# Scores inside the chunks of a gated linear recurrence: two full products for a pair of chunks in place of four partial ones

## The chip, the cores and the metric

The kernel runs on one core of a Trainium2 chip. The metric is the device time of one execution in microseconds (us). Before the change three runs gave 1615.14, 1615.44 and 1616.7 us, a median of 1615.44 us.

## The reference, cut to what matters

The kernel computes one encoder layer for 1024 tokens of width 1024, in float32: a recurrence branch with four heads, an attention branch with eight heads, a gated merge and a convolutional feed-forward network. The change lies in the recurrence, which runs over each head in both directions in chunks of 64 tokens:

```python
def gla_chunkwise(q, k, v, g):
    ...
    qd = q * jnp.exp(b)
    kd = k * jnp.exp(-b)
    A = jnp.einsum('bhncd,bhnsd->bhncs', qd, kd)
    mask = jnp.tril(jnp.ones((C, C), dtype=bool))
    A = jnp.where(mask, A, 0.0)
    intra = jnp.einsum('bhncs,bhnse->bhnce', A, v)
    ...
    inter = jnp.einsum('bhncd,bhnde->bhnce', qd, S_prev)
    return (intra + inter).reshape(B, H, L, dv)
```

A second call with the time axis flipped gives the backward direction, and the two results are added.

## The kernel before, in words

The program goes through stages: the first norm and two projections (to about 80 us), the recurrence of the four heads (`hg_proj` and `hg_rec`, to about 378 us), the rotary projections of the attention branch (`rope_unit`, names rk and rq), attention, the merge, and the feed-forward network with its down projection.

`hg_rec` (line 289) holds a head's tokens as eight pairs of chunks, 128 tokens each. For each direction it forms the scaled queries `qds[d]` and keys `kds[d]` (128 features by 1024 tokens), turns the keys round (`kt`, line 332), multiplies them with the values (`u`, line 338) and builds the states on VectorE (`R`, line 347, and `st`, line 349). Then come two blocks `b` of four pairs each. In each block TensorE forms the scores (lines 359 to 362), VectorE masks them and builds the 128 by 128 matrix `A` of each pair, which holds both directions (lines 365 to 370), and TensorE multiplies `A` with the values and adds the states' part in `po` (lines 376 and 378). A norm over `po` (`sq`, `hss`, `rs_h`, lines 379 to 386), a turn on TensorE (`ot`, line 389) and a copy (`oT`, line 390) end the block. There are four heads, so eight such blocks and 32 pairs.

The scores of a pair are four products before. Line 359 multiplies the backward keys of all 128 tokens with the backward queries of the first 64, line 360 the forward keys of all 128 with the forward queries of the last 64; both write the tile `a1`. Lines 361 and 362 multiply 64 keys with 64 queries: the forward direction inside the first chunk and the backward direction inside the second, into the two halves of the partitions of `a2`. The profile calls both tiles `a`. One product of the program in plain float32 is two loads and two matmuls in the profile.

The masked copies and sums on VectorE:

```python
V.copy_predicated(A, mask1..., a1.rearrange("p i a b -> p i (a b)"))
V.copy_predicated(at, mask2..., a2)
for r in (slice(0, CH), slice(CH, P)):
    V.tensor_tensor(out=A[r, :, r], in0=A[r, :, r], in1=at[r], op=ALU.add)
```

The tiles `kt`, `u`, `a1`, `a2` and `ot` share one tag "t" of three buffers in PSUM, so that each of them waits until the tile three places earlier has been read. The order of instructions on each engine is set when the program is built, by a scheduler that simulates the program on a timeline of its own; each engine then goes through its list in order. The work that stands between the steps of a head on TensorE is that of others: `hp` (line 92 to 94, the next head's projections), `v` and `sg` (values and gates), `gp` (line 257, branch gates of the attention stage) and `rk`.

At the end of the recurrence stands the rotary stage. Its projections `rk` take three PSUM buffers (tag "g"), and the fourth needs the first one back. For that ScalarE and VectorE have to copy out `rawk`, `sqk` and `vv` (lines 466, 468 and 77/78), and on VectorE the tables `cosq`, `cosk`, `sinq`, `sink` (lines 444 and 451) stand ahead of `vv`.

Of the kernel before, what the change touches and what calls it, by code (L numbers as in the profile page):

```python
# [10 lines left out]
F32 = mybir.dt.float32  # L11
# [6 lines left out]
P = 128  # L18
# [5 lines left out]
CH = 64  # L24
# [20 lines left out]
def hybrid_kernel(ctx: ExitStack, tc: tile.TileContext, x, gn, vec, cst, rope,  # L45
# [3 lines left out]
    V, S, T = nc.vector, nc.scalar, nc.tensor  # L49

    def pool(name, bufs, stack=ctx, **kw):
        return stack.enter_context(tc.tile_pool(name=name, bufs=bufs, reuse_waits="tile", **kw))
# [16 lines left out]
    mask1 = cs[:, C_M1:C_M1 + P].bitcast(U32)  # L69
    mask2 = cs[:, C_M2:C_M2 + CH].bitcast(U32)  # L70
# [147 lines left out]
    for d, (a, b) in enumerate(((V_LBF0, V_LBF1), (V_LBB0, V_LBB1))):  # L218
        w = slice(4 * d, 4 * d + 4)
# [16 lines left out]
    hps = pool("hps", 3, hg, space=PSUM)  # L236
# [52 lines left out]
    def hg_rec(h, q, ks, gs, vt, sg):  # L289
        e = slice((h % 2) * P, (h % 2 + 1) * P)  # L290
        chunks = lambda a: a.rearrange("p (a j) -> p a j", j=CH)
        first = lambda a: a.rearrange("p (a two j) -> p a two j", two=2, j=CH)[:, :, 0, :]
        qds, kds, decs = [], [], []
        for d in range(2):
            k, g = ks[d], gs[d]
            c = hp4.tile([P, L], F32, tag="c", name=f"c{h}{d}", bufs=2)
            for w in (slice(0, 512), slice(512, 1024)):
                V.tensor_tensor_scan(c[:, w], reset, g[:, w], 0.0, ALU.mult, ALU.add)
            tot = hp4.tile([P, 16], F32, tag="tot", name=f"tot{h}{d}", bufs=2)
            V.tensor_copy(tot, chunks(c)[:, :, CH - 1])  # L300
            c63 = tot.rearrange("p (a two) -> p a two", two=2)[:, :, 0:1].to_broadcast([P, 8, CH])
            if d == 0:
                b = c
                V.tensor_tensor(out=first(b), in0=first(c), in1=c63, op=ALU.subtract)
            else:
                b = g
                V.tensor_tensor(out=b, in0=g, in1=c, op=ALU.subtract)
                V.tensor_tensor(out=first(b), in0=first(b), in1=c63, op=ALU.add)
            dec = hp4.tile([P, 16], F32, tag="dec", name=f"dec{h}{d}", bufs=4)
            S.activation(dec, tot, AF.Exp)  # L310
            qd = hp3.tile([P, L], F32, tag="qd", name=f"qd{h}{d}", bufs=2)
            S.activation(qd, b, AF.Exp)
            V.tensor_tensor(out=qd, in0=qd, in1=q, op=ALU.mult)
            S.activation(b, b, AF.Exp, scale=-1.0)
            V.tensor_tensor(out=k, in0=k, in1=b, op=ALU.mult)
            qds.append(qd)
            kds.append(k)
            decs.append(dec)


        states = [[None] * NPAIR, [None] * NPAIR]
        for d in range(2):
            order = range(NPAIR) if d == 0 else range(NPAIR - 1, -1, -1)
            E0 = lambda p: decs[d][:, 2 * p + (1 if d else 0):2 * p + (1 if d else 0) + 1]
            E1 = lambda p: decs[d][:, 2 * p + (0 if d else 1):2 * p + (0 if d else 1) + 1]
            order = list(order)
            for b in range(2):
                grp = order[4 * b:4 * b + 4]
                pt = hps.tile([P, 4, P], F32, tag="t", name=f"kt{h}{d}{b}")
                kT = hp4.tile([P, 4, P], F32, tag="kT", name=f"kT{h}{d}{b}", bufs=2)  # L330
                for i, p in enumerate(grp):
                    T.transpose(pt[:, i, :], kds[d][:, p * P:(p + 1) * P], ident)
                S.copy(kT, pt)
                pu = hps.tile([P, 4, P], F32, tag="t", name=f"u{h}{d}{b}")
                for i, p in enumerate(grp):
                    if p == order[-1]:
                        break
                    T.matmul(pu[:, i, :], kT[:, i, :], vt[:, p, e], start=True, stop=True)
                for i, p in enumerate(grp):
                    if p == order[-1]:  # L340
                        break
                    nxt = order[4 * b + i + 1]
                    st = hp3.tile([P, P], F32, tag=f"st{d}", name=f"st{h}{d}{nxt}", bufs=8)
                    src = pu[:, i, :]
                    if states[d][p] is not None:
                        R = hp1.tile([P, P], F32, tag="R", name=f"R{h}{d}{p}", bufs=2)
                        V.tensor_tensor(out=R, in0=src, in1=states[d][p], op=ALU.add)
                        src = R
                    V.tensor_scalar(st, src, E1(p), E0(nxt), ALU.mult, ALU.mult)
                    states[d][nxt] = st  # L350

        oT = hp3.tile([P, L], F32, tag="oT", name=f"oT{h}", bufs=1)
        for b in range(2):
            a1 = hps.tile([P, 4, 2, CH], F32, tag="t", name=f"a1{h}{b}")
            a2 = hps.tile([P, 4, CH], F32, tag="t", name=f"a2{h}{b}")
            for i in range(4):
                o = (4 * b + i) * P
                w, f, s = slice(o, o + P), slice(o, o + CH), slice(o + CH, o + P)
                T.matmul(a1[:, i, 0, :], kds[1][:, w], qds[1][:, f], start=True, stop=True)
                T.matmul(a1[:, i, 1, :], kds[0][:, w], qds[0][:, s], start=True, stop=True)  # L360
                T.matmul(a2[0:CH, i, :], kds[0][:, f], qds[0][:, f], start=True, stop=True)
                T.matmul(a2[CH:P, i, :], kds[1][:, s], qds[1][:, s], start=True, stop=True)
            A = hp3.tile([P, 4, P], F32, tag="A", name=f"A{h}{b}", bufs=2)
            nc.gpsimd.memset(A, 0.0)
            V.copy_predicated(A, mask1.unsqueeze(1).to_broadcast([P, 4, P]),
                              a1.rearrange("p i a b -> p i (a b)"))
            at = a_tmp[b]
            V.copy_predicated(at, mask2.unsqueeze(1).to_broadcast([P, 4, CH]), a2)
            for r in (slice(0, CH), slice(CH, P)):
                V.tensor_tensor(out=A[r, :, r], in0=A[r, :, r], in1=at[r], op=ALU.add)  # L370
            po = hps.tile([P, 4, P], F32, tag="o", name=f"po{h}{b}", bufs=2)
            for i in range(4):
                p = 4 * b + i
                w = slice(p * P, (p + 1) * P)
                inter = [(qds[d][:, w], states[d][p]) for d in range(2) if states[d][p] is not None]
                T.matmul(po[:, i, :], A[:, i, :], vt[:, p, e], start=True, stop=False)
                for n, (a, s) in enumerate(inter):
                    T.matmul(po[:, i, :], a, s, start=False, stop=n == len(inter) - 1)
            sq = hp4.tile([P, 4, P], F32, tag="sq", name=f"sq{h}{b}")
            S.activation(sq, po, AF.Square)  # L380
            ss = hp4.tile([P, 4], F32, tag="ss", name=f"hss{h}{b}", bufs=2)
            V.tensor_reduce(out=ss, in_=sq, axis=AX.X, op=ALU.add)
            r = rstd_of(hp4, ss, P, 4, f"h{h}{b}")
            for i in range(4):
                V.scalar_tensor_tensor(out=sq[:, i, :], in0=po[:, i, :], scalar=r[:, i:i + 1],
                                       in1=sg[:, 4 * b + i, e], op0=ALU.mult, op1=ALU.mult)
            pt = hps.tile([P, 4, P], F32, tag="t", name=f"ot{h}{b}")
            for i in range(4):
                T.transpose(pt[:, i, :], sq[:, i, :], ident)
            S.activation(oT[:, b * 512:(b + 1) * 512], pt.rearrange("p a b -> p (a b)"), AF.Copy,  # L390
                         scale=vc[:, V_ON:V_ON + 1])
        nc.sync.dma_start(oa_d[h], oT)
# [23 lines left out]
    at = ExitStack()  # L416
# [22 lines left out]
    for n, col, sc in (("q", V_QG, HD ** -0.5), ("k", V_KG, 1.0)):  # L439
# [3 lines left out]
        s = rp.tile([P, 8, HD], F32, name=f"sin{n}")  # L443
# [173 lines left out]
    for h in range(HG_HEADS):  # L617
        t = slot_p(f"oal{h}", F32)
# [20 lines left out]
    for c in range(KT):  # L639
        wh, wl = weight_block(wab[c], f"ab{c}")  # L640
        sgt = []
        for n in range(2):
            t = slot_q(f"gl{n}{c}", F32)
# [3 lines left out]
        for half in range(2):  # L647
            w = slice(half * 512, (half + 1) * 512)
            for n in range(2):
                ps = yps.tile([P, 512], F32, tag="y", name=f"y{c}{half}{n}")  # L650
                for k in range(4):
                    kw = slice((4 * n + k) * P, (4 * n + k + 1) * P)
                    h, l = oab[4 * n + k]
# [71 lines left out]
    A, B, C, C1, C2, U2 = {}, {}, {}, {}, {}, {}  # L725
# [18 lines left out]
    def m1(j):  # L744
        A[j] = bank_a(f"pa{j}")
        product(A[j], wa[j], 0, "b11", True)

    def m2(j):
        B[j] = bank_b(f"pb{j}")
        product(B[j], wa[j], 1, "b21", True)  # L750
# [186 lines left out]
    for i in range(2):  # L937
        r = wpool.tile([P, 2, NH], F32, tag="raw", name=f"left{i}")
# [178 lines left out]
```

## Time and profile before

| what | value |
|---|---|
| median of three runs | 1615.44 us |
| time of the profiled execution | 1616.18 us |
| span of the profiled execution, first to last instruction | 1614.3 us |
| TensorE matmul busy | 1579.3 us, 98% |
| TensorE weight loads busy | 1334.1 us, 83% |
| VectorE busy | 1112.5 us, 69% |
| ScalarE busy | 768.0 us, 48% |
| mean granted TensorE clock | 0.993 of full |

The span is what the profile covers; the time of the execution is 1.88 us longer. Busy shares are means over stages with different limits, so a stage has to be read by itself. Matmuls overlap each other in the profile: what one costs is the step from its start to the start of the next, not its own duration.

### The profile page before, as it was taken

The page shows a single profiled execution, that of the slowest core. Times are in us where ns is not written, and L with a number is a line of the kernel's source. Part 1 is how long each engine was busy: PE and PEld are TensorE (multiplying, and loading weights), DVE is VectorE, ACT ScalarE, POOL GpSimd, SP SyncE. Part 2 cuts the span into 40 slices and gives each one's busy share as a digit, 9 for nine tenths or more (in the row PEclk, how much of TensorE's full clock was granted, in tenths as well). Part 3 has the DMA queues.
Part 4 walks back from the last instruction along what each step waited for, and adds up shares of the span by engine and source line. Part 5 has one row for each costly group of instructions (what it writes and reads, how often), then busy time and mean ns, then how long its engine had stood idle before and what let it go on. Part 6 is the DMA issues. An engine that isn't in the chain of part 4 may idle for free.

```text
span 1614.3 us, 21171 instructions
## 1 busy us (share of the span) xinstructions
PE 1579.3 (98%) x8376; PEld 1334.1 (83%) x8376; DVE 1112.5 (69%) x1632; ACT 768.0 (48%) x1204; POOL 35.3 (2%) x33
## 2 busy tenths in 40 slices
PE   8999999999999999999999989999999999999998
PEld 7988998888988888888788877788788888787887
DVE  5366465534758888888654288887888777967576
ACT  5375454513555666656432344544544444444432
POOL 0000000000000000000000052000000000000000
PEclk9999999999999999999999999999999999999999
DMA  5011111121110101102445111322222224685343
GB/s 204 27 41 38 53 40 49 64 78 54 46 60 27 46 33 40 47 26 99 167 140 195 53 59 66 104 98 98 98 98 98 103 106 147 212 296 186 100 122 104
DMA packets 59764, 150.34 MB, mean 93 GB/s; under 512 B 6161, under 2 KB 6417, under 8 KB 59666
## 3 DMA queue, kind: packets, MB, share of 16 engines
q1 hardware_dynamic: 59666, 148.99, 26.9%
q8 instruction: 66, 1.08, 0.3%
q14 instruction: 32, 0.26, 0.1%
HBM read 109.91 MB, written 39.06 MB: 92 GB/s over the span
## 4 chain that ended last, share of the span: by engine, by line
PE 85%; DVE 6%; DMA 5%; ACT 3%; issue 1%; SPq 0%; DVEq 0%; ACTq 0%
PE pa L741 13%; PE gp L257 10%; PE pc L741 6%; PE pv L578 4%; PE pb L741 3%; PE pt L567 3%; PE s L547 2%; PE hp L93 2%; PE s L548 2%; PE hp L94 2%; PE hp L92 2%; PE y L93 2%; PE y L94 2%; PE y L92 2%; PE wo L94 2%; PE wo L93 2%
## 5 line engine op out<-in xcount | busy, mean ns | idle before, releaser
L77 ACT CAST pth<-pt 128x512 fp32r<-128x512 f32 x128 | 71.1, 589 | 77.8 <-PE pt L567 77.5
L77 ACT CAST dz<-dr 128x512 fp32r<-128x512 f32 (+1 forms) x66 | 50.6, 767 | 102.1 <-PE da L94 35.8
L78 DVE TENSOR_TENSOR dz<-dr,dz 128x512 fp32r<-128x512 f32 (+1 forms) x66 | 56.9, 867 | 50.8 <-ACT dz L77 50.6
L78 DVE TENSOR_TENSOR ptl<-pt,pth 128x512 fp32r<-128x512 f32 x128 | 84.0, 683 | 10.3 <-ACT pth L77 9.9
L257 PE MATMUL gp<-uT1h,w_g 128*128 128x512 f32 x256 | 86.9, 398 | 0.0
L257 PE MATMUL gp<-uT0h,w_g 128*128 128x512 f32 x256 | 86.4, 400 | 0.0
L550 DVE TENSOR_REDUCE m<-s 128x1 f32<-128x1024 f32 x64 | 78.3, 1224 | 7.3 <-PE s L548 6.3
L553 ACT ACTIVATE p<-s,m 128x1024 f32<-128x1024 f32 x64 | 72.1, 1127 | 19.7 <-DVE m L550 19.7
L741 PE MATMUL pc<-c1t,wb 128*128 128x512 f32 x264 | 69.5, 398 | 5.5 <-ACT c1t L77 5.0
L741 PE MATMUL pa<-c0b,wa 128*128 128x512 f32 x264 | 68.9, 394 | 2.8 <-ACT wa L77 1.7
L741 PE MATMUL pb<-c0b,wa 128*128 128x512 f32 x264 | 68.7, 390 | 0.5 <-DVE ta L714 0.5
L567 PEld LDWEIGHTS pt<-cs,p 128*128 128x128 f32 x512 | 58.7, 140 | 12.0 <-issue 4.8
L741 PE MATMUL pa<-c1t,wb 128*128 128x512 f32 x264 | 67.9, 395 | 0.0
L567 PE MATMUL pt<-cs,p 128*128 128x128 f32 x512 | 66.9, 273 | 0.5 <-DVE p L555 0.5
L578 PE MATMUL pv<-pth,vv 128*128 128x256 f32 x256 | 65.1, 292 | 0.0
L741 PEld LDWEIGHTS pc<-c1t,wb 128*128 128x128 f32 x264 | 50.5, 192 | 17.0 <-ACT c1t L77 5.2
L77 ACT CAST wc<-r 128x1024 fp32r<-128x1024 f32 x22 | 23.1, 1052 | 86.1 <-PE pc L741 76.4
L578 PE MATMUL pv<-ptl,vv 128*128 128x256 f32 x256 | 62.5, 282 | 0.0
L741 PEld LDWEIGHTS pa<-c0b,wa 128*128 128x128 f32 x264 | 49.0, 188 | 15.4 <-ACT wa L77 3.2
L741 PEld LDWEIGHTS pa<-c1t,wb 128*128 128x128 f32 x264 | 50.1, 190 | 12.0 <-DVE c1t L78 0.4
L741 PEld LDWEIGHTS pb<-c0b,wa 128*128 128x128 f32 x264 | 49.5, 188 | 11.4 <-DVE ta L714 0.9
L868 DVE SCALAR_TENSOR_TENSOR cv<-c,vc,cv 128x1023 f32<-128x1023 f32 x44 | 56.3, 1279 | 2.6 <-ACT cv L867 2.6
(461 smaller groups left out, 4578.1 us busy)
## 6 DMA issues: line engine op xcount, KB each, us to landing
r<-in_wup_dram SPq DMA_DIRECT2D x44, 512.0 KB, 3.3
left_d<-cv SPq DMA_DIRECT2D x33, 512.0 KB, 3.2
dr<-left_d SPq DMA_DIRECT2D x66, 256.0 KB, 2.7
raw_g<-in_win_f_dram SPq DMA_DIRECT2D x16, 512.0 KB, 3.2
gate_d<-gt SPq DMA_DIRECT2D x32, 256.0 KB, 2.0
gl<-gate_d SPq DMA_DIRECT2D x16, 512.0 KB, 4.0
raw_h<-in_win_f_dram SPq DMA_DIRECT2D x12, 512.0 KB, 3.3
w<-in_wdown_dram SPq DMA_DIRECT2D x20, 256.0 KB, 5.4
```

The costliest lines, as they stand in the source:

```text
L77: S.copy(h, src)
L78: V.tensor_tensor(out=l, in0=src, in1=h.bitcast(F32), op=ALU.subtract)
L92: T.matmul(ps, ah, bh, start=first, stop=False, skip_group_check=more)
L93: T.matmul(ps, ah, bl, start=False, stop=False, skip_group_check=more)
L94: return T.matmul(ps, al, bh, start=False, stop=last, skip_group_check=more)
L257: yield T.matmul(ps, a[:, w], b[:, k, :], start=k == 0 and n == 0, stop=k == KT - 1 and n == 2)
L550: V.tensor_reduce(out=m, in_=s, axis=AX.X, op=ALU.max, negate=True)
L553: S.activation(pb, s, AF.Exp, bias=m, accum_out=z)
L567: pin(T.transpose(pt[:, i, :], pb[:, k * P:(k + 1) * P], ident))
L578: pin(T.matmul(pv, vv[pair // 2][:, k, :], pts[u][k // 4][n][:, k % 4, :, :], start=k == 0 and n == 0, stop=k == KT - 1 and n == 1))
L741: T.matmul(ps, a[:, k * P:(k + 1) * P], x[:, k, :], start=first and n == 0, stop=n == len(seq) - 1, skip_group_check=not first)
L868: V.scalar_tensor_tensor(out=cv[:, 1:], in0=src[:, :-1], scalar=w0, in1=cv[:, 1:], op0=ALU.mult, op1=ALU.add)
```

## The change

For each pair the four products become two, each with all 128 keys and all 128 queries: one of the backward direction into the tile `ab`, one of the forward direction into `af`. Each of the two tiles fills a buffer of 128 by 4 by 128; `a1` was as large, `a2` half of that. The masked copies read the parts that they need from them: two copies of 128 by 256 in place of one of 128 by 512, and two of 64 by 256 in place of one of 128 by 256. The two sums stay. What is computed beyond the old four products (the forward scores of later keys for the first chunk's queries, and the backward scores of the earlier keys for the second's) is not read.

```diff
-            a1 = hps.tile([P, 4, 2, CH], F32, tag="t", name=f"a1{h}{b}")
-            a2 = hps.tile([P, 4, CH], F32, tag="t", name=f"a2{h}{b}")
+            af, ab = (hps.tile([P, 4, P], F32, tag="t", name=f"a{d}{h}{b}") for d in range(2))
             for i in range(4):
-                o = (4 * b + i) * P
-                w, f, s = slice(o, o + P), slice(o, o + CH), slice(o + CH, o + P)
-                T.matmul(a1[:, i, 0, :], kds[1][:, w], qds[1][:, f], start=True, stop=True)
-                T.matmul(a1[:, i, 1, :], kds[0][:, w], qds[0][:, s], start=True, stop=True)
-                T.matmul(a2[0:CH, i, :], kds[0][:, f], qds[0][:, f], start=True, stop=True)
-                T.matmul(a2[CH:P, i, :], kds[1][:, s], qds[1][:, s], start=True, stop=True)
+                w = slice((4 * b + i) * P, (4 * b + i + 1) * P)
+                T.matmul(ab[:, i, :], kds[1][:, w], qds[1][:, w], start=True, stop=True)
+                T.matmul(af[:, i, :], kds[0][:, w], qds[0][:, w], start=True, stop=True)
+
             A = hp3.tile([P, 4, P], F32, tag="A", name=f"A{h}{b}", bufs=2)
             nc.gpsimd.memset(A, 0.0)
-            V.copy_predicated(A, mask1.unsqueeze(1).to_broadcast([P, 4, P]),
-                              a1.rearrange("p i a b -> p i (a b)"))
             at = a_tmp[b]
-            V.copy_predicated(at, mask2.unsqueeze(1).to_broadcast([P, 4, CH]), a2)
-            for r in (slice(0, CH), slice(CH, P)):
+            f, s = slice(0, CH), slice(CH, P)
+            m1 = lambda w: mask1[:, w].unsqueeze(1).to_broadcast([P, 4, CH])
+            m2 = lambda r: mask2[r].unsqueeze(1).to_broadcast([CH, 4, CH])
+            V.copy_predicated(A[:, :, f], m1(f), ab[:, :, f])
+            V.copy_predicated(A[:, :, s], m1(s), af[:, :, s])
+            V.copy_predicated(at[f], m2(f), af[f, :, f])
+            V.copy_predicated(at[s], m2(s), ab[s, :, s])
+            for r in (f, s):
                 V.tensor_tensor(out=A[r, :, r], in0=A[r, :, r], in1=at[r], op=ALU.add)
```

The scheduler sets the order anew. The lists of the engines stay the same but for shifts of some instructions inside the recurrence and up to the first rotary projections, and a few places among the products of the merge. Three places matter here.

The first is TensorE at the first block of the first head, where its scores follow the last `u` (`u011` is the `u` of head 0, direction 1, second group; `a100` and `a200` are the tiles `a1` and `a2` of head 0, block 0). Before, the first rows of the block:

```order
L338 MATMUL u011_1082<-vt0_122,kT011_1076 128x128 x2
L359 MATMUL a100_1099<-qd01_995,k01_784 128x64 [waits PE_49]
L360 MATMUL a100_1099<-qd00_981,k00_783 128x64
L361 MATMUL a200_1100<-qd00_981,k00_783 64x64 [waits DVE_49]
L362 MATMUL a200_1100<-qd01_995,k01_784 64x64
```

After the change (here `a000` is `af` and `a100` is `ab`), the whole block:

```order
L338 MATMUL u011_1082<-vt0_122,kT011_1076 128x128 x2
L357 MATMUL a100_1100<-qd01_995,k01_784 128x128 [waits PE_49]
L358 MATMUL a000_1099<-qd00_981,k00_783 128x128 [waits DVE_49]
L357 MATMUL a100_1100<-qd01_995,k01_784 128x128
L358 MATMUL a000_1099<-qd00_981,k00_783 128x128
L357 MATMUL a100_1100<-qd01_995,k01_784 128x128
L358 MATMUL a000_1099<-qd00_981,k00_783 128x128
L357 MATMUL a100_1100<-qd01_995,k01_784 128x128
L358 MATMUL a000_1099<-qd00_981,k00_783 128x128
```

Sixteen products have become eight, and the wait for VectorE, which stood behind two products, now stands behind one.

The second is VectorE at the same block. Before:

```order
L347 TENSOR_TENSOR R011_1095<-u011_1082,st011_1090 128x128 [waits DVE_49]
L349 TENSOR_SCALAR st010_1094<-R011_1095,dec01_993 128x128 [waits DVE_49]
L365 COPY_PREDICATED A00_1117<-cs_80,a100_1099 128x512 [waits PE_49,Pool_49]
L368 COPY_PREDICATED atmp0_778<-cs_80,a200_1100 128x256 [waits PE_49]
L370 TENSOR_TENSOR A00_1117<-A00_1117,atmp0_778 64x4x64 [waits DVE_49]
```

After:

```order
L366 COPY_PREDICATED A00_1109<-cs_80,a100_1100 128x4x64 [waits PE_49,Pool_49]
L347 TENSOR_TENSOR R011_1095<-u011_1082,st011_1090 128x128 [waits DVE_49]
L369 COPY_PREDICATED atmp0_778<-cs_80,a100_1100 64x256
L367 COPY_PREDICATED A00_1109<-cs_80,a000_1099 128x4x64 [waits PE_49]
L368 COPY_PREDICATED atmp0_778<-cs_80,a000_1099 64x256
L349 TENSOR_SCALAR st010_1094<-R011_1095,dec01_993 128x128 [waits DVE_49]
```

Two masked copies have become four, and the last `R` and `st` stand between and behind them.

The third is ScalarE at the first rotary projections, behind the last block of the last head. Before:

```order
L466 COPY rawk_3267<-rk_3335 128x2x64 [waits PE_49]
L468 ACTIVATE sqk_3361<-rk_3335 128x128 [waits DVE_49]
L390 ACTIVATE oT_2794<-ot_2895,vc 128x512 [waits PE_49]
L77 CAST vv<-rk_3269 128x64
L77 CAST vv<-rk_3302 128x64
```

After:

```order
L467 COPY rawk0_3219<-rk2_3287 128x2x64 [waits PE_49]
L391 ACTIVATE oT3_2758<-ot31_2847,vc_81 128x512 [waits PE_49]
L469 ACTIVATE sqk2_3313<-rk2_3287 128x128 [waits DVE_49]
L77 CAST vv_3180<-rk0_3221 128x64
L77 CAST vv_3180<-rk1_3254 128x64
```

The copy `oT`, which waits for the turn `ot`, has moved ahead of the squares `sqk` of the third projection.

## Rows read from the trace of the kernel before

**Rows 1.** The page: busy time by engine, and the chain of waits by engine.
```profile
PE 1579.3 (98%) x8376; PEld 1334.1 (83%) x8376; DVE 1112.5 (69%) x1632; ACT 768.0 (48%) x1204; POOL 35.3 (2%) x33
...
PE 85%; DVE 6%; DMA 5%; ACT 3%; issue 1%; SPq 0%; DVEq 0%; ACTq 0%
```

**Rows 2.** Busy time by stretch: the recurrence, and the entry of the rotary stage.
```profile
core 0: us, PE busy (x) PEld busy (x) DVE busy (x) ACT busy (x) POOL busy (x), PEclk, DMA share, GB/s
120.00:378.00 258.00, 257.53 (x1663) 228.59 (x1662) 136.09 (x263) 114.03 (x145) 3.35 (x6) 1.00 0.16 56
378.00:390.00 12.00, 8.04 (x48) 7.83 (x48) 4.91 (x22) 2.88 (x14) 0.00 (x0) 0.72 0.12 46
```

**Rows 3.** Timeline of TensorE, first block's scores (start, duration, engine, line, shapes, count).
```profile
126.67 0.33 PE L359 MATMUL a<-qd,k 128*128 128x64 f32 x2
126.84 0.39 PE L360 MATMUL a<-qd,k 128*128 128x64 f32 x2
127.67 0.27 PE L361 MATMUL a<-qd,k 128*64 128x64 f32 x1 [0.45 <-DVE R L347]
...
127.94 0.43 PE L359 MATMUL a<-qd,k 128*128 128x64 f32 x2
128.21 0.39 PE L360 MATMUL a<-qd,k 128*128 128x64 f32 x2
128.53 0.27 PE L361 MATMUL a<-qd,k 128*64 128x64 f32 x1
...
130.50 0.50 PE L93 MATMUL hp<-uT1l,w_h 128*128 128x512 f32 x1
```

**Rows 4.** Timeline of TensorE: products of 128 by 128 with 128 columns.
```profile
119.67 1.06 PE L338 MATMUL u<-vt,kT 128*128 128x128 f32 x8
120.57 0.60 PE L332 MATMUL kt<-cs,k 128*128 128x128 f32 x4
...
137.21 0.39 PE L376 MATMUL po<-vt,A 128*128 128x128 f32 x2
137.43 0.61 PE L378 MATMUL po<-st,qd 128*128 128x128 f32 x4
137.88 0.39 PE L376 MATMUL po<-vt,A 128*128 128x128 f32 x2
```

**Rows 5.** VectorE's instructions of lines 365, 368 and 370 (min/median/max ns).
```profile
L365 DVE COPY_PREDICATED A<-cs,a x8: 729/738/749, 130.4 to 366.3; 128x512 f32<-128x512 uint32 x8
L368 DVE COPY_PREDICATED atmp<-cs,a x8: 426/430/436, 131.0 to 366.9; 128x256 f32<-128x256 uint32 x8
L370 DVE TENSOR_TENSOR A<-A,atmp x16: 417/420/424, 131.5 to 367.8; 64x256 f32<-64x256 f32 x16
```

**Rows 6.** Timeline: last sums of the first head's two blocks on VectorE, and their `po`.
```profile
131.50 0.85 DVE L370 TENSOR_TENSOR A<-A,atmp 64x256 f32<-64x256 f32 x2
151.46 0.85 DVE L370 TENSOR_TENSOR A<-A,atmp 64x256 f32<-64x256 f32 x2
...
136.77 0.38 PE L376 MATMUL po<-vt,A 128*128 128x128 f32 x2
154.50 0.39 PE L376 MATMUL po<-vt,A 128*128 128x128 f32 x2
```

**Rows 7.** Timeline at the entry of the rotary stage: ScalarE, VectorE, TensorE.
```profile
378.65 0.28 ACT L468 ACTIVATE sqk<-rk 128x128 f32<-128x128 f32 x1
378.93 0.69 ACT L390 ACTIVATE oT<-ot,vc 128x512 f32<-128x512 f32 x1
379.51 0.43 ACT L77 CAST vv<-rk 128x64 fp32r<-128x64 f32 x3
...
378.97 0.29 DVE L469 TENSOR_REDUCE ssk<-sqk 128x2 f32<-128x128 f32 x1 [1.79 <-ACT sqk L468]
379.17 0.68 DVE L444 TENSOR_TENSOR cosq<-cos,tgq 128x512 f32<-128x512 f32 x1
...
381.99 0.98 DVE L78 TENSOR_TENSOR vv<-rk,vv 128x64 fp32r<-128x64 f32 x6
...
378.29 0.60 PE L389 MATMUL ot<-cs,sq 128*128 128x128 f32 x4
382.86 0.55 PE L92 MATMUL rk<-w_kv,uT0h 128*128 128x256 f32 x1 [3.96 <-DVE vv L78]
```

## The prediction

> **What bounds the kernel now.** I read the page first: TensorE is busy for 98% of the span, and it holds 85% of the chain that ended last [rows 1]. That is a mean over stages, so the second view is the busy time of the stretch in which the change lies. From 120 to 378 us TensorE is busy for 257.53 of 258.00 us, at full clock, while VectorE works for 136.09 and ScalarE for 114.03 us [rows 2]. The reader is to see that in the recurrence TensorE has no gap to speak of: whatever is taken from its list there comes off the end, as long as nothing else becomes late. The third view is TensorE's timeline at a block of scores, because overlapping matmuls show durations that are longer than what they cost; the step from start to start is the cost. The fourth is the place where TensorE does wait: the entry of the rotary stage, where it stands still for 3.96 us [rows 7].
>
> **What is taken from TensorE.** In the first block the scores of the second pair start at 127.94 us, and the work behind the block starts at 130.50 us [rows 3]. Between them lie three pairs, so a pair costs 2.56 / 3 = 0.853 us. Inside it the two products with 64 columns take 0.27 us (line 359, 127.94 to 128.21) and 0.32 us (line 360, 128.21 to 128.53), and the two small ones together 0.26 us. So a product with half the columns, and even a small one that runs beside another, costs 0.26 to 0.32 us in this place.
>
> **What is added to TensorE.** A full product (128 keys, 128 columns, plain float32) is what `po` already consists of. Six of its matmul instructions start between 137.21 and 137.88 us [rows 4], so one costs 0.67 / 6 = 0.1117 us, and a product, being two of them, 0.223 us. The eight of `u` between 119.67 and 120.57 us give 0.1125 us. The new pair is then 4 x 0.1117 = 0.447 us. The bounds: no row of such a product is cheaper than 0.11 us; the dearest row that could apply is the step of 0.32 us for line 360's product above, which would make the pair 0.64 us. I take the `po` rows, because they have the same shape and types and alternate between sources as the new scores do. The gain of a pair is 0.853 - 0.447 = 0.406 us, of 32 pairs 13.0 us (at the dear bound 0.213 x 32 = 6.8 us).
>
> A full product is cheaper than one with half its columns in these rows, so the columns do not set the price. The Trainium skill (TensorE: Matmul & The Clock Gate, section on LDWEIGHTS) says that loading the stationary operand costs its column count at 1.2 GHz, whatever the contraction. By it 128 columns take an estimated 107 ns, a new pair four loads or 0.427 us, and the gain would be 13.6 us; the trace's 0.1117 us for a whole step agrees, and I keep the trace's.
>
> **What is given back on TensorE.** First, the wait in the first block. Before, the first two products (126.67 to about 127.22 us) lay ahead of the wait for `R`, and TensorE went on at 127.67 us [rows 3]. Now only one product stands ahead of that wait, as the order shows. Since VectorE's list up to that `R` is unchanged, TensorE again goes on at 127.67 us, and seven products of 0.223 us then end at 129.23 us in place of 130.50 us. This block gains 1.27 us, not 4 x 0.406 = 1.62 us: 0.35 us are lost. In the other blocks the `R` that is waited for lies behind a stretch of filler work, and no such wait stands in the trace.
>
> Second, the entry of the rotary stage. There `oT` has moved ahead of the third `sqk` on ScalarE. Before, `sqk` started at 378.65 us, and `oT`, which has to wait for `ot`, at 378.93 us; `ssk`, `cosq`, the other tables and `vv` followed on VectorE, and TensorE was released at 382.86 us [rows 7]. Now `oT` starts at about the same distance from `ot`, and `sqk` takes the place that the `vv` cast had behind it, 379.51 us on the old scale: 0.86 us later. VectorE's list from `ssk` to `vv` is a plain sequence without slack, so TensorE's wait of 3.96 us becomes about 4.8 us. I charge 0.86 us. If `ot` ends so early that `oT` is through when the third projection ends, this is 0; it cannot be much more, since only `oT` is moved.
>
> **What is added to VectorE, and what hides it.** Before, a block costs 738 + 430 + 2 x 420 = 2008 ns there [rows 5]. The four new copies have 256 elements in each partition, as line 368 has, so each is 430 ns: 4 x 430 + 840 = 2560 ns, 552 ns more in a block and 4.4 us in all. Reading every other run of 64 columns is not in the trace; I bound it by line 365's 738 ns for 512 elements: for the two copies that do so 2 x 308 ns more, 1.2 us a block in all. What hides it is the filler between the scores and `po`. In the first block the sums end at 131.50 + 0.85 = 132.35 us and `po` starts at 136.77 us, 4.4 us later; five of the other blocks are alike. The tightest is the second block of the first head: sums until 152.31, `po` at 154.50 us, 2.2 us [rows 6]. There VectorE's copies wait for its own earlier work, which moves forward by only the 1.27 us of the first block, while TensorE also saves this block's 1.62 us; with 0.55 us more copying and about one filler instruction more, some 0.5 to 1 us of cover is left. I cost VectorE's part at nothing. Without that cover it would be at most 0.55 us a block.
>
> GpSimd's clearing of `A`, the DMA queues' order and the three PSUM buffers stay as they are.
>
> **The sum.** 13.0 - 0.35 - 0.86 = 11.8 us. The profiled execution took 1616.18 us (span 1614.3 and 1.88 us around it), which becomes 1604.4 us. It lies 0.74 us above the median of the three runs, 1615.44 us; on that median the forecast is **1603.6 us**, 0.7% faster.
>
> **The rivals.**
>
> *The columns count after all, and it is slower.* Counted in columns, a pair is 64 + 64 + 64 before (the two small products run side by side) and 128 + 128 after. Were the price in this place one per column, 0.853 x 256 / 192 = 1.137 us, the 32 pairs would cost 9.1 us more: 1624.5 us. It decides from 0.853 / 4 = 0.213 us for one full matmul instruction. For it: products that are half empty should not cost full price. The Trainium skill says the like: TensorEngine Tiling (Array Packing), under its theoretical speedup, gives up to twofold for a free dimension of 64 or less, which speaks for small products and against this change. Against it: `po` and `u` pay 0.112 us for exactly this shape [rows 4], and the half-wide products pay more than that [rows 3]. By that rule, the trace disagrees already. 3%.
>
> *The other engines become the bound.* With 13 us less work on TensorE between the same steps of VectorE and ScalarE, the chain from projection to states to `po` may run out of filler, and TensorE waits. For it: VectorE gets 4.4 us more, and the second block has little cover. Against it: VectorE and ScalarE are busy for about half of the stretch, and in the new order the scores are followed by more filler, not less. If half of the gain goes so, it is 1609.5 us; a loss of 3 to 5 us gives 1607 to 1609 us (12% for a loss in part). If all of it goes, the time is that of before, 1615.4 us (5%).
>
> *The clock at the rotary entry.* From 378 to 390 us the granted clock is 0.72, that is 2.4 GHz for some of it and 1.2 GHz for the rest, after TensorE had stood still for 3.96 us [rows 2, 7]. That costs about 0.28 x 12 = 3.4 us. If the halt comes shorter, or the clock does not fall, these come as well: 1600.2 us. The wait gets longer by my sum, so I hold it for less likely: 14%.
>
> **How the numbers follow.** The forecast has 66% and by itself spans 1602 to 1606 us. The low end of the range takes in the clock rival, 1599.6 us; the high end the dear bound of the product's price with the same deductions (1615.44 - 6.8 + 1.2 = 1609.8 us) nearly, and the partial loss to the other engines: I set 1608.8 us. A measurement of this kernel can tell about 0.2%, 3.2 us, from no change, so the cases up to 1612.2 us are faster: 66 + 14 + 12 = 92%; same 5%; slower 3%.
>
> **What would show it.** Right: TensorE's timeline shows a pair of scores in about 0.45 us (four instructions, 0.11 us from start to start), and a block in about 1.8 us; TensorE is busy without gaps from 120 to about 366 us, and the rotary stage is entered some 12 us earlier; the wait there reads about 4.8 us on `vv`; VectorE's four copies read about 430 ns each. Wrong: a step of over 0.16 us between the new products, a TensorE wait for `A` ahead of `po`, or a wait for `kT` or `st` that was not there. A halt of under 3 us at the rotary entry, or a clock of 1.00 from there on, would show the clock rival.

## The result and the profile after

Four runs of the changed kernel gave 1600.18 to 1603.25 us, a median of 1601.96 us; four of the kernel before gave 1614.64 to 1616.7 us, a median of 1615.29 us. The ratio is 0.9916, with a 95% interval of 0.9898 to 0.9933: faster by 13.3 us, where 11.8 us were forecast. The profiled execution took 1600.18 us, with a span of 1598.1 us.

The page's busy times and its chain by engine, of the changed kernel:

```profile
PE 1562.5 (98%) x8248; PEld 1322.0 (83%) x8248; DVE 1115.0 (70%) x1648; ACT 767.9 (48%) x1204; POOL 35.1 (2%) x33
...
PE 85%; DVE 6%; DMA 4%; ACT 3%; issue 1%; SPq 0%; DVEq 0%; ACTq 0%
```

The shares stand where they stood [rows 1]: TensorE still bounds the kernel, with 128 matmul instructions fewer, and VectorE's busy time grows by 2.5 us.

TensorE's timeline at the first block of scores, to be read against [rows 3]:

```profile
125.90 0.39 PE L357 MATMUL a<-qd,k 128*128 128x128 f32 x2
126.90 0.49 PE L358 MATMUL a<-qd,k 128*128 128x128 f32 x2 [0.61 <-DVE R L347]
127.22 0.39 PE L357 MATMUL a<-qd,k 128*128 128x128 f32 x2
127.44 0.39 PE L358 MATMUL a<-qd,k 128*128 128x128 f32 x2
127.67 0.39 PE L357 MATMUL a<-qd,k 128*128 128x128 f32 x2
...
128.48 0.47 PE L93 MATMUL hp<-uT1l,w_h 128*128 128x512 f32 x1
```

A pair steps from 127.22 to 127.67 us, 0.45 us in place of 0.853 us. TensorE goes on from the wait at 126.90 us and leaves the block at 128.48 us, 1.58 us for seven products; before it was 127.67 to 130.50 us, 2.83 us. Everything here lies 0.77 us earlier than before, because the first stage of this execution was that much shorter (the `u` ahead of the block starts at 125.23 in place of 126.00 us); the wait itself ends at the same place in VectorE's work.

VectorE's four copies (min/median/max ns; line 366 is 365 of before cut in two, and so on):

```profile
L366 DVE COPY_PREDICATED A<-cs,a x8: 437/446/453, 128.6 to 354.0; 128x256 f32<-128x256 uint32 x8
L367 DVE COPY_PREDICATED A<-cs,a x8: 444/446/451, 129.8 to 354.9; 128x256 f32<-128x256 uint32 x8
L368 DVE COPY_PREDICATED atmp<-cs,a x8: 426/430/434, 130.1 to 355.3; 64x256 f32<-64x256 uint32 x8
L369 DVE COPY_PREDICATED atmp<-cs,a x8: 447/449/458, 129.3 to 354.5; 64x256 f32<-64x256 uint32 x8
```

The sum is 1771 ns where lines 365 and 368 took 1168 ns [rows 5], 603 ns more in a block and 4.8 us in eight. VectorE's busy time on the page grows by less, since instructions that overlap are counted once there and others took a little less. The copies that write only 64 partitions cost as much as those that write 128.

The entry of the rotary stage, ScalarE, VectorE and TensorE, against [rows 7]:

```profile
365.43 0.69 ACT L391 ACTIVATE oT<-ot,vc 128x512 f32<-128x512 f32 x1 [0.17 <-PE ot L390]
366.01 0.27 ACT L469 ACTIVATE sqk<-rk 128x128 f32<-128x128 f32 x1
...
366.32 0.29 DVE L470 TENSOR_REDUCE ssk<-sqk 128x2 f32<-128x128 f32 x1 [1.43 <-ACT sqk L469]
366.52 0.68 DVE L445 TENSOR_TENSOR cosq<-cos,tgq 128x512 f32<-128x512 f32 x1
...
369.34 0.98 DVE L78 TENSOR_TENSOR vv<-rk,vv 128x64 fp32r<-128x64 f32 x6
...
364.79 0.60 PE L390 MATMUL ot<-cs,sq 128*128 128x128 f32 x4
370.20 0.55 PE L92 MATMUL rk<-w_kv,uT0h 128*128 128x256 f32 x1 [4.81 <-DVE vv L78]
```

`oT` now stands ahead of the third `sqk`, and TensorE's wait is 4.81 us where it was 3.96 us. From the first block's `u` to the release of `rk` the kernel before took 382.86 - 126.00 = 256.86 us, the changed one 370.20 - 125.23 = 244.97 us: the recurrence and its way out are 11.9 us shorter.

### The profile page after: what moved, and what is told of

Read it like the earlier page. It is cut to its first block, busy times and chain, and to the rows that moved or that the text cites. A ratio compares the mean times of both kernels' runs of the same rounds, so it can differ in the third digit from the quotient of the medians.

```text
span 1598.1 us, 20940 instructions
## 1 busy us (share of the span) xinstructions
PE 1562.5 (98%) x8248; PEld 1322.0 (83%) x8248; DVE 1115.0 (70%) x1648; ACT 767.9 (48%) x1204; POOL 35.1 (2%) x33
## 4 chain that ended last, share of the span: by engine, by line
PE 85%; DVE 6%; DMA 4%; ACT 3%; issue 1%; SPq 0%; DVEq 0%; ACTq 0%
PE pa L742 14%; PE gp L257 10%; PE pc L742 6%; PE pv L579 4%; PE pt L568 3%; PE pb L742 3%; PE s L548 2%; PE y L92 2%; PE s L549 2%; PE y L93 2%; PE hp L93 2%; PE hp L94 2%; PE y L94 2%; PE hp L92 2%; PE wo L94 2%; PE wo L93 2%
```

## The experiments

**VectorE's part alone.** The four partial products stay and are written into the full-size tiles; the masked copies are those of the change.

```diff
...
-                T.matmul(ab[:, i, :], kds[1][:, w], qds[1][:, w], start=True, stop=True)
-                T.matmul(af[:, i, :], kds[0][:, w], qds[0][:, w], start=True, stop=True)
+                T.matmul(ab[:, i, 0:CH], kds[1][:, w], qds[1][:, f], start=True, stop=True)
+                T.matmul(af[:, i, CH:P], kds[0][:, w], qds[0][:, s], start=True, stop=True)
+                T.matmul(af[0:CH, i, 0:CH], kds[0][:, f], qds[0][:, f], start=True, stop=True)
+                T.matmul(ab[CH:P, i, CH:P], kds[1][:, s], qds[1][:, s], start=True, stop=True)
```

> The four partial products stay, written into the full-size tiles; VectorE makes the four masked copies of the change. So VectorE's part of the change stands alone. Theory (the gain is TensorE's, VectorE's part is hidden): a pair of scores still costs 0.85 us on TensorE, VectorE works 0.55 us more in a block, and the time is that of before within 0.2% (1614 to 1617 us). Rival (VectorE's 4.4 us lie on the path): 1618 to 1620 us.

Measured: 1617.03 us beside 1615.71 us of the kernel before, ratio 1.0005 with an interval of 0.9995 to 1.0015. TensorE's timeline of this kernel, from the second to the third pair of the first block:

```profile
126.50 0.43 PE L358 MATMUL a<-qd,k 128*128 128x64 f32 x2
127.35 0.43 PE L358 MATMUL a<-qd,k 128*128 128x64 f32 x2
```

A pair still steps by 0.85 us. So the gain is not in the copies, which leaves the products. What the copies cost is too small to be told: the median lies at the upper end of the theory's range, and the interval reaches from 0.8 us less to 2.4 us more than before. In the profile the way from the `u` ahead of the first block to the release of `rk` takes 259.13 us in place of 256.86 us; 0.85 us of that is the rotary entry, where `oT` stands first here too, and the rest was not taken apart.

**Full products cut by columns.** `o` is the first token of the pair. Twice the weight loads of the change, the same columns, no half-size product.

```diff
...
-                T.matmul(ab[:, i, :], kds[1][:, w], qds[1][:, w], start=True, stop=True)
-                T.matmul(af[:, i, :], kds[0][:, w], qds[0][:, w], start=True, stop=True)
+                for d, z in ((1, ab), (0, af)):
+                    for c in (slice(0, CH), slice(CH, P)):
+                        T.matmul(z[:, i, c], kds[d][:, w], qds[d][:, o + c.start:o + c.stop], start=True, stop=True)
```

> Each full product is cut in two by its columns: all 128 keys against 64 queries, four products a pair, the same 256 columns as the change and twice its weight loads, no half-size products. Theory (each matmul instruction with 128 keys costs one step of about 0.11 us, whatever its columns): a pair costs 8 x 0.1117 = 0.89 us, 0.45 us more than in the change, 32 pairs 14.3 us more, so about 1616 us, no faster than before. Rival 1 (the columns set the price): 0.45 us a pair, about 1602 us. Rival 2 (the price of before came from going to and fro between full and half-size products): about 0.45 us a pair and about 1602 us as well.

Measured: 1615.19 us beside 1615.71 us, ratio 0.9997 (0.9988 to 1.0006). TensorE's timeline of this kernel at the first block:

```profile
126.85 0.56 PE L360 MATMUL a<-qd,k 128*128 128x64 f32 x4
127.85 3.34 PE L360 MATMUL a<-qd,k 128*128 128x64 f32 x28 [0.45 <-DVE R L347]
131.00 0.48 PE L93 MATMUL hp<-uT1l,w_h 128*128 128x512 f32 x1
```

28 instructions step through 127.85 to 131.00 us, 0.1125 us each, for 64 columns; the change pays 1.58 / 14 = 0.113 us for 128. The whole gain is gone although no half-size product is left. So a matmul instruction with 128 keys takes the same step with 64 columns as with 128, and both rivals are out for this kernel. The run does not show that going between full and half-size products was free in the kernel before: a pair has only four instructions with 128 keys there, 0.45 us by this price, and four in the change as well. The other 0.40 us of its 0.853 us belong to the half-size products, and the next run helps to divide them.

**Full products cut by keys.** The halves can run side by side.

```diff
...
-                T.matmul(ab[:, i, :], kds[1][:, w], qds[1][:, w], start=True, stop=True)
-                T.matmul(af[:, i, :], kds[0][:, w], qds[0][:, w], start=True, stop=True)
+                for d, z in ((1, ab), (0, af)):
+                    for c in (slice(0, CH), slice(CH, P)):
+                        T.matmul(z[c, i, :], kds[d][:, o + c.start:o + c.stop], qds[d][:, w], start=True, stop=True)
```

> Each full product is cut in two by its keys: 64 keys against 128 queries, each half to its own 64 partitions of the result, four products a pair. Two halves can run side by side, as the small products of before did. Theory (from before's rows: two small products side by side took 0.26 to 0.27 us in company of full ones): a pair costs 0.45 to 0.54 us, 0 to 3 us more in all than the change, 1602 to 1606 us. Rival (halves side by side are worth twofold): 0.25 us a pair, 6 us less than the change, about 1596 us. If they do not run side by side: 0.89 us a pair, about 1616 us.

Measured: 1605.76 us beside 1615.71 us, ratio 0.9937 (0.9922 to 0.9952). At the first block:

```profile
126.87 0.44 PE L360 MATMUL a<-qd,k 128*64 128x128 f32 x4
127.76 1.75 PE L360 MATMUL a<-qd,k 128*64 128x128 f32 x28 [0.45 <-DVE R L347]
129.44 0.50 PE L93 MATMUL hp<-uT1l,w_h 128*128 128x512 f32 x1
```

28 instructions in 1.68 us are 0.060 us each, 0.48 us for a pair of eight, the steps into and out of the run of halves included. Inside it two halves start together every 0.109 us (at 128.03, 128.14 and 128.25 us). So two halves do run side by side, at the price of one whole: cutting a full product so brings nothing here, and it does not bring twofold. The pair is as the theory had it; the rival's 0.25 us is out. The time is 3.7 us over the change's two medians, a little more than the theory's 0 to 3 us. In the profiles 3.2 us of the distance to the change lie behind the release of `rk` (1231.1 us from there to the end in place of 1227.9 us), where the program is the same; the rest was not taken apart.

The two runs together also take the pair of before apart, as an estimate. Its four instructions with 128 keys cost 4 x 0.1125 = 0.45 us and its four half-size ones 4 x 0.060 = 0.24 us when no other size stands between them, 0.69 us in all. (The halves of this run have 128 columns; those of before have 64, and two couples of them start as far apart, at 128.53 and 128.63 us.) The remaining 0.16 us are, by this working, the price of mixing the sizes. Rows 3 show where it falls: the two steps of line 359, at the return to the full size, take 0.27 us and the two of line 360, up to the first half-size product, 0.32 us, where the run cut by columns takes 0.225 us for two. Of the 0.406 us that a pair gains, then, about 0.24 us are the half-size products themselves and about 0.16 us the mixing. No run has the products of before in an order that mixes less, so this share is worked out and not tested by itself.

**The backward products first.**

```diff
-            for i in range(4):
-                w = slice((4 * b + i) * P, (4 * b + i + 1) * P)
-                T.matmul(ab[:, i, :], kds[1][:, w], qds[1][:, w], start=True, stop=True)
-                T.matmul(af[:, i, :], kds[0][:, w], qds[0][:, w], start=True, stop=True)
+            for z, d in ((ab, 1), (af, 0)):
+                for i in range(4):
+                    w = slice((4 * b + i) * P, (4 * b + i + 1) * P)
+                    T.matmul(z[:, i, :], kds[d][:, w], qds[d][:, w], start=True, stop=True)
```

> The four backward products of a block come first, then the four forward ones, instead of in turn. Theory (in the first block of the first head the forward tile waits for VectorE's R, at a moment that VectorE sets): four products instead of one lie ahead of the wait, which falls from 0.61 us to under 0.1 us in the profile; the time is that of the change, 1600 to 1603.5 us, since half a microsecond cannot be seen in it. Rival (the wait belongs to the first product behind the states whatever it is): it stays at 0.6 us or so.

Measured: one run of 1601.5 us. The block has no wait in it any more:

```profile
126.54 2.13 PE L358 MATMUL a<-qd,k 128*128 128x128 f32 x16
128.43 0.48 PE L93 MATMUL hp<-uT1l,w_h 128*128 128x512 f32 x1
```

The block takes 1.89 us from its start, where the change took 125.90 to 128.48 us, 2.58 us. The wait was the forward tile's, and it can be hidden behind the backward products. In the time of the whole kernel it does not show, as expected.

**The change again.**

> The change itself, unaltered, beside the others on the same chip. Every theory: 1600 to 1603.5 us, 13 to 14 us under the kernel before.

Measured: 1602.11 us (1598.99 to 1604.15) beside 1616.09 us, ratio 0.9911 (0.9894 to 0.9928). The wait at the rotary entry was 4.81 us again.

**The rotary tables on GpSimd.**

```diff
-    for n, col, sc in (("q", V_QG, HD ** -0.5), ("k", V_KG, 1.0)):
+    for n, col, sc in (("k", V_KG, 1.0), ("q", V_QG, HD ** -0.5)):
...
-        V.tensor_tensor(out=c, in0=cos, ...)
+        nc.gpsimd.tensor_tensor(out=c, in0=cos, ...)
...
-                V.tensor_tensor(out=sv, in0=nv, ...)
+                nc.gpsimd.tensor_tensor(out=sv, in0=nv, ...)
...
```

> The change, and the rotary tables (cosq, cosk, sinq, sink) are made by GpSimd instead of VectorE, the keys' tables first. Theory (at the entry of the rotary stage TensorE waits for vv, and vv waits behind the third sqk and then behind 2.8 us of tables on VectorE): the wait of 4.8 us falls to about 2 us, and the clock loss behind it may go as well: 2.8 to 5 us off the change, 1596.5 to 1599.5 us. Rival 1 (the casts of vv on ScalarE or the recurrence's end hold it anyway): the wait stays above 4 us and the time is that of the change. Rival 2 (GpSimd is so slow that the keys' rotation has to wait for its tables): a new wait later, the time that of the change or longer.

Measured: 1598.32 us (1597.28 to 1599.48) beside 1616.09 us, ratio 0.9889 (0.9875 to 0.9904), 3.8 us under the change in the same series. VectorE and TensorE at the entry, then GpSimd's tables:

```profile
367.81 0.29 DVE L470 TENSOR_REDUCE ssk<-sqk 128x2 f32<-128x128 f32 x1 [1.43 <-ACT sqk L469]
368.02 0.98 DVE L78 TENSOR_TENSOR vv<-rk,vv 128x64 fp32r<-128x64 f32 x6
...
366.29 0.60 PE L390 MATMUL ot<-cs,sq 128*128 128x128 f32 x4
368.88 0.47 PE L92 MATMUL rk<-w_kv,uT0h 128*128 128x256 f32 x1 [1.99 <-DVE vv L78]
...
366.03 1.28 POOL L445 TENSOR_TENSOR cosk<-cos,tgk 128x512 f32<-128x512 f32 x1 [68.28 <-DVE tgq L442]
368.48 1.71 POOL L452 TENSOR_TENSOR sink<-sin,tgk 128x128 f32<-128x128 f32 x4
```

`vv` now follows `ssk` at once, and the wait falls from 4.81 to 1.99 us, the 2.8 us of tables. The other 1 us of the gain in time is not accounted for. GpSimd needs about twice VectorE's time for a table and nobody waits for it. This shows the chain that the prediction built its 0.86 us on: `sqk`, `ssk`, the tables and `vv` in one file, with TensorE at its end.

**Both together.**

> The change with the tables on GpSimd and the four backward products first. Theory: the gains of the two add, about 3 to 5.5 us off the change, 1596 to 1599 us. Rival: one of the two brings nothing beside the other, then the better one alone.

Measured: 1597.99 us (1596.96 to 1603.1) beside 1616.09 us, ratio 0.9893 (0.9875 to 0.9912). It is level with the tables alone; half a microsecond cannot be told here. By the medians either version is faster than the change (1602.11 us) and than the kernel before (1616.09 us); against the change the intervals of the ratios still overlap.

**The copies made twice.**

```diff
             V.copy_predicated(at[s], m2(s), ab[s, :, s])
+            V.copy_predicated(A[:, :, f], m1(f), ab[:, :, f])
+            V.copy_predicated(A[:, :, s], m1(s), af[:, :, s])
+            V.copy_predicated(at[f], m2(f), af[f, :, f])
+            V.copy_predicated(at[s], m2(s), ab[s, :, s])
```

> The change with its four masked copies made twice, 1.8 us more work for VectorE in each of the eight blocks, 14 us in all; it serves to show where VectorE's cover ends. Theory (cover of 0.93 us in the second block of the first head, about 2 us in the last block and 3.7 us or more in the others): 0 to 1.5 us over the change, 1601 to 1604 us. Rival (VectorE's copies lie on the path): up to 14 us over the change, 1610 to 1616 us.

Measured: 1607.15 us beside 1616.09 us, ratio 0.9946 (0.9929 to 0.9962), 5.0 us over the change. Neither expectation holds. The theory had also read the cover of the change wrongly: it is 0.82 us in the fourth block and 2.8 to 3.3 us in two others, not 3.7 us or more. In the profile one wait is new, in the last block of the last head:

```profile
PE rk L92 <- DVE vv L78: 4.7, 1, 4.7
...
PE ot L394 <- ACT rawk L471: 2.5, 1, 2.5
```

The sums of `A` still end ahead of `po`, since the scheduler put more `rk` between them. But only three projections, 72 instructions, can run before the buffers are used up, and so none were left to cover the norm between `po` and `ot`. In the other seven blocks the extra work of VectorE makes no new wait. The new wait is 2.5 us, and the profiled execution, at 1602.20 us the fastest of the four, is 1.7 us over that of the change in the same series. That the rest of the 5.0 us is clock, which was 0.992 to 0.994 in the three other runs, is argued, not shown.

## Why the prediction was right, point by point

**The price of a product.** The prediction took 0.1117 us for a matmul instruction from `po`, 0.447 us for a pair; the profile shows 0.45 us. The experiment with half columns shows why the shape of `po` was the right row: 64 columns cost 0.1125 us as well. The rule of the Trainium skill (TensorE: Matmul & The Clock Gate, LDWEIGHTS), an estimated 107 ns for 128 columns of weights, agrees within 6% with the 0.1117 us of `po`, the 0.1125 us with 64 columns and the 0.113 us of the change. The price of before, 0.853 us, was taken from the timeline as a whole. The prediction did not say why half-wide products cost so much there; by the experiments they cost no more than full ones by themselves, and the surplus is the half-size products and the mixing.

**The first block.** 1.27 us of gain were forecast, 0.35 us less than in a free block, and 2.83 - 1.58 = 1.25 us came. The wait stood behind one product, at the moment that VectorE's `R` sets; the run with the backward products first removed it.

**The rotary entry.** 0.86 us were charged for `oT` ahead of `sqk`. The wait grew from 3.96 to 4.81 us. The runs give more than one pair for this: the scheduler left `sqk` first in the two runs with cut products, and there the wait is 3.96 us; it put `oT` first in the run with the copies alone, in the one with the backward products first and in both profiles of the change, and there it is 4.81 us. In these seven profiles the wait goes with the order, whatever the products are.

**VectorE's cover.** 0.5 to 1 us were expected in the tightest block. In the profile of the change the second block of the first head has its sums and `po` so:

```profile
149.46 0.87 DVE L371 TENSOR_TENSOR A<-A,atmp 64x256 f32<-64x256 f32 x2
...
151.26 0.39 PE L377 MATMUL po<-vt,A 128*128 128x128 f32 x2
```

The sums end at 150.33 us, 0.93 us ahead of `po`. Three of the four copies cost 16 to 19 ns more than the 430 ns taken, so that a block costs 603 ns more in place of 552; line 368 costs 430 ns, though it too reads only every other run of 64 columns. The cover held it. But the tightest block after the change is another one, the second block of the second head:

```profile
212.34 0.39 DVE L371 TENSOR_TENSOR A<-A,atmp 64x256 f32<-64x256 f32 x1
...
213.55 0.38 PE L377 MATMUL po<-vt,A 128*128 128x128 f32 x2
```

The sums end 0.82 us ahead of `po`, where the kernel before had 4.4 us and the prediction counted this block among those with room. They end at 212.73 us, as they did before (212.72 us), while `po` has come forward from 217.12 to 213.55 us: VectorE did not move forward with TensorE here. That this cover would hold was not worked out beforehand, and was in part luck.

**The sum** of 11.8 us is what the stretch shows, 11.9 us. The time moved by 13.3 us in one series and 14.0 us in the other. The median of 1601.96 us lies at the low edge of the 1602 to 1606 us that the forecast was given. The surplus goes with the clock. The run results list the mean granted clock: 0.993 to 0.995 in 26 runs of the kernel before, 0.994 to 0.997 in the eight of the change. In the series of **The change again** runs of the change at 0.997 took 1598.99 and 1600.51 us, those at 0.994 took 1603.70 and 1604.15 us; in the series of the result three runs at 0.997 took 1600.18 to 1602.27 us. At an equal 0.994 the kernel before has a median of 1615.73 us (13 runs), so that the difference at the same clock is 11.8 us, from two runs of the change. Two of the places can be seen; the first fence is of before, the second of the change (the ninth number, behind the engines' busy times, is the clock):

```profile
380.00:390.00 10.00, 7.14 (x40) 7.18 (x41) 3.88 (x20) 1.42 (x8) 0.00 (x0) 0.66 0.14 55
470.00:480.00 10.00, 10.00 (x43) 8.09 (x42) 5.38 (x8) 4.44 (x8) 0.00 (x0) 0.83 0.14 49
```

```profile
370.00:380.00 10.00, 9.80 (x71) 9.83 (x72) 4.36 (x16) 2.39 (x11) 0.00 (x0) 0.84 0.01 2
460.00:470.00 10.00, 10.00 (x55) 8.33 (x54) 7.24 (x12) 4.94 (x9) 0.00 (x0) 1.00 0.07 27
```

At the rotary entry 1.6 us of full clock are lost (10 us times 1 - 0.84) in place of 3.4 us, and the later dip of 1.7 us is absent. The prediction had this as a rival with 14%, for the entry alone, if the halt came shorter or the clock did not fall. The halt grew longer and the loss smaller all the same. The length of the halt does not settle it in these profiles: with the same 3.96 us the 10 us in which it ends lost 3.4 us in the kernel before and in the run cut by keys (clock 0.66), but 1.7 us in the run cut by columns (0.83); with 4.81 us they lost 3.4 us in the run with the copies alone (0.66), and 1.6 us here. The later dip is back in the profile with the backward products first (0.83 from 450 to 460 us). That the surplus is clock is worked out from these figures, and no run sets the clock by itself. So the 1.5 to 2.2 us over the sum were luck for the kernel and no part of the mechanism. Why the changed kernel met the lower clock less often is open: no run here was made to tell it.

**The rivals.** That columns set the price is refuted by the run with half columns. That VectorE and ScalarE take the gain back did not happen: apart from the two waits charged for and one of 0.8 us for `kT` that is the same before and after, TensorE waits nowhere in the recurrence; the run with doubled copies and the fourth block's 0.82 us show how near it is. The clock, above, came in part, and beside the forecast, not in its place.

## What to carry to other kernels

In these runs a plain float32 product with 128 stationary columns took one step of about 0.112 us per matmul instruction, with 64 moving columns as with 128. Before cutting a product to spare its masked half, count the instructions and the changes between full and half size, not the multiplied elements. When work is taken off the engine that bounds a stage, read the new order at the places where that engine waits for a file of small instructions on another; there a copy that changes places can give back a microsecond, and an idle engine can take work out of that file. The length of the filler that is left (the products of other stages that stand between two steps of a head) says how much the other engines may grow, and it has to be read in every block: the tightest one after a change need not be the tightest before.

## What had not been expected of the hardware

Two half-height products of 64 stationary columns each, side by side, step at 0.060 us an instruction, a little more than half of the 0.1125 us of the full-height one: side by side they make up for their number and no more. Mixed with full ones, as in the kernel before, a pair of scores cost about 0.16 us more than these prices add up to. A masked copy of 256 elements costs 430 to 449 ns on 64 partitions as on 128, and the one of 512 elements 738 ns, so that cutting that one in two added 154 ns here (446 + 446 ns).
